# Sample units in another order, value transposes asked for later, and the order of the halves at the start of the output projection

## The chip, the cores and the metric

The kernel runs on one core of one Trainium2 chip. The metric is the device time of one execution in microseconds; of several runs the median is given. The profile is of one more execution, whose own time stands beside its span below.

The core's engines as the profile names them: PE is TensorE (matmuls, PEld its weight loads), DVE VectorE, ACT ScalarE, POOL GpSimd, SP SyncE, which only issues transfers. Each works through its own list of instructions in order and waits at the head of that list.

## The reference, cut to what matters

One decoder layer for two groups of requests that share the weights: a prompt of 1024 tokens and 8 samples of 8 new tokens with a cache of 4096 tokens each. The part around the change is attention and the output projection:

```python
k_cmp = rms_norm(compress(full[:, :, 0], ...), k_gain[0]); v_cmp = compress(full[:, :, 1], ...)
o_cmp, p_cmp = cmp_attention(q, k_cmp, v_cmp, q_pos)
top_i, sel_ok = select_blocks(p_cmp, q_pos, -(-full.shape[1] // SLC_BLOCK))
o_slc = slc_attention(q, top_i, sel_ok, q_pos, full[:, :, 2], full[:, :, 3])
o_win = window_prompt(...)      # or window_sample(...) over the last 512 tokens and the new ones
o_attn = g[..., 0:1] * o_cmp + g[..., 1:2] * o_slc + g[..., 2:3] * o_win
x = x + gate1 * (jnp.concatenate([o_attn, y_conv, y_pool], axis=-1) @ w_out)
h = rms_norm(x, norm2) * (1 + scale2) + shift2
x = x + gate2 * swiglu(h, w_up, w_down)
```

Everything is float32; large products are made of three matmuls on high and low halves.

## The kernel before

The program is written as Python generators, one for each task, and a small planner (`run`, `spawn`, `hold`). The planner keeps an estimated time for each engine (`self.t`, advanced by `use`, `mm` and `tr`). A generator yields the time from which it can go on; of those that can, the planner takes the one with the lowest priority number. This sets the order in which the program is traced. A scheduler with its own model of the engines then sets each engine's list from the traced order and the dependences; `issue_after(x)` adds an edge, so that what is traced inside it comes behind `x` on the engine of `x`.

Three stages follow one another. In the first (to about 370 us) the modulation and the input projection run. In the second, attention, these tasks share TensorE: the last batches of `compress` (the samples' compressed keys and values), the prompt's attention, and the samples' attention. The third (from about 830 us) is the output projection, then the feed-forward part, up and down.

**Prompt attention.** There are 32 units: eight blocks of 128 queries, two halves of the heads, and a branch each (selected with compressed, or window). `scores` (L1078) forms the scores in PSUM, moves them with the mask to `P` on VectorE (L1131), takes the exponential on ScalarE (L1143), and scales by gate and sum on GpSimd (L1153). At its end it spawns `values` (L1161) with the planner's time `ready` at which the last scaling is done. `values` transposes `P` on TensorE in pieces (L144, tile `ident,P`), moves them out as `pt`, and multiplies by the values. The output of a block and half leaves as `mo` (L1223). There are two `P` tiles, and a unit's scores start only when the values of the unit before the last are done (`v_done >= u - 1`).

**Sample attention.** There are 36 units: four pairs of samples, nine units each. Units x = 0 to 7 of a pair are eight parts of the cache, masked by the pair's selected blocks; x = 8 is the sliding window. A unit has a 1 MB tile of keys and values: for x < 8 eight loads of 128 KB each, whose pages come from the page table (L532), for x = 8 one load of 1 MB (L1360). The tiles rotate through two buffers `unit`, and three more, `stream`, from the time when `compress` has given them up; `sample_load` loads the next unit whenever a unit is done. `sample_attention` (L1365) holds a unit until the pair's selection is there (`"at" in st`, set by `sample_select`), then forms scores (`unit,qb` or `stream,qb`), minimum and exponential (`e`); `sample_values` transposes `e` (`ident,e`), moves it to `spt` and multiplies by the values (`unit,spt`, `stream,spt`); the result goes into column `nx` of `part`: 0 to 7 for the selected parts, 9 for the window, 8 and 10 for the new tokens, 11 for the compressed branch. After a pair's ninth unit `sample_combine` (L1427) joins the columns to `co`. For the fourth pair the last step, `sample_store`, happens inside the output projection, at its third weight tile.

**Output projection** (L1540). Eight weight tiles of 512 KB (`w_raw`, three buffers, L1537) are split into high and low halves (`w_hi` on ScalarE, L176; `w_lo` on VectorE or GpSimd, L172). The mixed activations are taken in four quarters of 272 tokens; a quarter is loaded in four pairs of rows (`pair`, L1500 for the first quarter, L1567 for the others) and split into `mh` and `ml` (L176, L172). The groups are quarter 0, quarter 1, then quarters 2 and 3 together; each goes through all eight weight tiles, 24 matmuls a tile and quarter. `mix` splits one pair of rows; the first four belong to the first quarter. `w_raw` lies where `stream` and other tiles of the attention stage lay.

Of the kernel before, what the change touches and what calls it, by code (L numbers as in the profile page):

```python
# [8 lines left out]
F32R = mybir.dt.float32r  # L9
# [8 lines left out]
P = 128  # L18
# [8 lines left out]
HALF = 272  # L27
# [36 lines left out]
class Kernel:  # L64
# [1013 lines left out]
    def scores(self, pool, u, j, half, br):  # L1078
# [10 lines left out]
        if br == "slc":  # L1089
            kj, off = 0, (0 if j < 7 else 64)  # L1090
            seg = [(1, 64 - off, ns)] + ([(0, 0, nc_)] if j < 7 else [])
            lo, hi, mask, m0 = off, 64 + ns, self.m_slc, SEQ - ns - 64
        else:
            kj, off = 1, 64 + w0
            seg = [(2, 0, nw)] + ([(0, nw, nc_)] if j == 7 else [])
            lo, hi = 64 + w0, 64 + ns
# [14 lines left out]
        ready = 0.0  # L1111
        K = self.K[kj]
        for hl in range(2):
# [42 lines left out]
                self.first_evac = self.last_evac  # L1156
                self.scored = True
            yield 0.0
        self.spawn(0, self.values(pool, u, j, half, br, Pt, seg, ready + 0.1))

    def values(self, pool, u, j, half, br, Pt, seg, ready):  # L1161

# [189 lines left out]
            self.unit_next += 1  # L1352

    def sample_fetch(self, u, kv):
        p, x = divmod(u, 9)
        if x < 8:
            for b2 in range(2):
                at = self.gather(kv[:, 4 * b2:4 * b2 + 4], "cacheB", 2 * p + b2, 4 * x, 4)
        else:
            self.nc.sync.dma_start(kv.rearrange("p (b t) f -> p b t f", b=2),  # L1360
                                   self.i["swinKV"][2 * p:2 * p + 2].rearrange("b p t f -> p b t f"))
            at = self.use("dma", 2.9, self.t["pe"]) + 2.5
        return kv.rearrange("p (b t) f -> p b t f", b=2), at

    def sample_attention(self, pool):  # L1365
        nc = self.nc
        self.loads = {}
        self.unit_free = ["unit"] * 2
        self.stream_left = True
        self.unit_next = 0  # L1370
        self.sample_load(pool)
        sts = [{} for _ in range(4)]
        self.spawn(1, self.sample_select(pool, 0, sts[0]))
        for u in range(36):
            p, x = divmod(u, 9)
            st = sts[p]
            if x == 0 and p < 3:
                if p > 0:
                    yield from self.hold(lambda: self.combined >= p)
                self.spawn(1, self.sample_select(pool, p + 1, sts[p + 1]))  # L1380
            yield from self.hold(lambda: "at" in st and u in self.loads and self.u_done >= u - 1)
            kv, at, src = self.loads.pop(u)
            yield max(at, st["at"])
            S = yield from self.bank_of("S")
            for b2 in range(2):
                self.mm(S[self.rows(b2), 0:512], self.qb[:, 2 * p + b2], kv[:, b2, :, 0:P], True, True)
            e = pool.tile([P, 512], F32, name="e", bufs=2)
            nx = x if x < 8 else 9
            v = lambda a: a.rearrange("p (j k) -> p j k", k=64)
            if x < 8:  # L1390
                i1 = st["bias"][:, 8 * x:8 * x + 8][:, :, None].to_broadcast([P, 8, 64])
                nc.vector.tensor_tensor_reduce(out=v(e), in0=v(S[:, 0:512]), in1=i1, scale=-1.0, scalar=3e38,
                                               op0=OP.add, op1=OP.min, accum_out=st["nm"][:, nx:nx + 1])
            else:
                nc.vector.tensor_tensor_reduce(out=e, in0=S[:, 0:512], in1=self.m_win, scale=-1.0, scalar=3e38,
                                               op0=OP.add, op1=OP.min, accum_out=st["nm"][:, nx:nx + 1])
            t = self.use("dve", 0.63, self.t["pe"] + 0.1)
            self.give("S", t)
            nc.scalar.activation(e, e, AF.Exp, scale=-1.0, bias=st["nm"][:, nx:nx + 1],
                                 accum_out=st["den"][:, nx:nx + 1])  # L1400
            t = self.use("act", 0.36, t + 0.1, table="exp")
            self.spawn(2, self.sample_values(pool, u, st, kv, e, nx, t + 0.2, src))
            yield 0.0
# [23 lines left out]
    def sample_combine(self, pool, st, p):  # L1427
        nc = self.nc
        nm, den, part, gr = st["nm"], st["den"], st["part"], st["gr"]

        w = pool.tile([P, 12], F32, name="cw", bufs=2)
        ds_ = pool.tile([P, 4], F32, name="cs", bufs=2)
        dd = pool.tile([P, 12], F32, name="cd", bufs=2)
        br = ((0, 9), (9, 11))
        for x, (a, b) in enumerate(br):
            nc.vector.tensor_reduce(ds_[:, x:x + 1], nm[:, a:b], axis=AX.X, op=OP.min)
        for x, (a, b) in enumerate(br):
            nc.scalar.activation(w[:, a:b], nm[:, a:b], AF.Exp, scale=-1.0, bias=ds_[:, x:x + 1])
        nc.vector.tensor_tensor(dd[:, 0:11], w[:, 0:11], den[:, 0:11], op=OP.mult)
        for x, (a, b) in enumerate(br):  # L1440
            nc.vector.tensor_reduce(ds_[:, 2 + x:3 + x], dd[:, a:b], axis=AX.X, op=OP.add)
        nc.vector.reciprocal(ds_[:, 2:4], ds_[:, 2:4])
        nc.vector.tensor_tensor(ds_[:, 2:4], ds_[:, 2:4], gr[:, 1:3], op=OP.mult)
        for x, (a, b) in enumerate(br):
            nc.vector.tensor_scalar(w[:, a:b], w[:, a:b], ds_[:, 2 + x:3 + x], None, op0=OP.mult)
        o = pool.tile([P, P], F32, name="co", bufs=2) if p < 3 else self.co
        nc.vector.tensor_scalar(o, part[:, 11], gr[:, 0:1], None, op0=OP.mult)
        for c in range(11) if p < 3 else (8, 10, 0, 1, 2, 3, 4, 5, 6, 7, 9):
            nc.vector.scalar_tensor_tensor(o, part[:, c], w[:, c:c + 1], o, op0=OP.mult, op1=OP.add)
        r = self.use("dve", 4.0, self.t["pe"]) + 0.5  # L1450
        if p < 3:
            yield r
            tr = yield from self.bank_of("S")
            self.sample_store(p, tr, o, pool.tile([P, 4, 2, NT], F32, name="smo", bufs=2))
            self.give("S", self.t["dve"])
        self.combined = p + 1
# [83 lines left out]
    def output_projection(self, wp, pool, nt, x1, opened):  # L1540
# [13 lines left out]
        def split():  # L1554
            if raw:
                t, at = raw.pop(0)
                with self.tc.issue_after(self.mix_hi.ins) if self.mix_hi else ExitStack():
                    ws.append([self.piece(wp, self.halves(t[:, x * 512:x * 512 + 512]), at, None) for x in range(2)])
# [11 lines left out]
        def mix(n=1):  # L1570
            for _ in range(n):
                c, k0, t, at = mx.pop(0)
                for k in range(2):
                    hi = pool.tile([P, HALF], F32R, name="mh", bufs=17)
                    lo = pool.tile([P, HALF], F32R, name="ml", bufs=17)
                    r = self.split(hi, lo, t[:, k], HALF, at)
                    parts[c, k0 + k] = (hi, lo, r)

        load()
        load()  # L1580
        split()
        mix(4)
        self.mix_hi = self.last_hi
        load()
# [808 lines left out]
```

## Time and profile before

| | us |
|---|---|
| median of 3 runs (1670.16 to 1675.92) | 1673.87 |
| the profiled execution | 1668.49 |
| its span, first to last instruction | 1666.9 |
| matmuls busy | 1568.7 |
| VectorE busy | 1089.8 |
| ScalarE busy | 779.4 |
| GpSimd busy | 657.6 |

Mean granted TensorE clock over the span: 0.976. The page's slices (40 of 41.7 us each) show TensorE busy at 0.9 or more nearly everywhere but in the first slice; the attention stage is slices 10 to 20:

```profile
PE   6999999998999799988799989999999999899998
PEld 2899997887777466665599979999999999899998
DVE  4713325884645677667489878776777776477767
ACT  3522215335666677656466534443434443344444
POOL 3111011123332233223013366554554555688765
PEclk9999999998999899999899999999999999999999
DMA  9586574425555624233596655446434335977653
```

A row of the view of stretches has the length, then for each engine the busy time with the number of instructions in brackets, the granted clock, the share of the transfer engines that is busy, and GB/s. A row of the order of time has start, duration, engine, line, operation, output and inputs, shape and count, and in brackets the idle time before it and what ended it.

### The profile page before, as it was taken

The numbers are of one execution on the slowest core, as the hardware profiler recorded it, in microseconds if no ns is written. First come the engines' busy times: TensorE is split into PE (matmuls) and PEld (weight loads), VectorE is DVE, ScalarE is ACT, GpSimd is POOL, SyncE is SP. The second block draws the span as 40 slices with busy tenths as digits, with TensorE's granted clock in tenths as the row PEclk, the third lists the DMA queues.
The fourth block names the chain that finished last, engine by engine and source line by source line (L and its number), as shares of the span: only waits on it lengthen the run. The fifth ranks groups of instructions, "written<-read, shape, count | busy, mean of one in ns | idle before, by whom it ended". The sixth has DMA issues, their size and how long they took to land.

```text
span 1666.9 us, 35454 instructions
## 1 busy us (share of the span) xinstructions
PE 1568.7 (94%) x12569; PEld 1390.2 (83%) x12569; DVE 1089.8 (65%) x2641; ACT 779.4 (47%) x1829; POOL 657.6 (39%) x791
## 2 busy tenths in 40 slices
PE   6999999998999799988799989999999999899998
PEld 2899997887777466665599979999999999899998
DVE  4713325884645677667489878776777776477767
ACT  3522215335666677656466534443434443344444
POOL 3111011123332233223013366554554555688765
PEclk9999999998999899999899999999999999999999
DMA  9586574425555624233596655446434335977653
GB/s 342 189 290 173 171 214 150 161 69 163 179 178 169 207 77 131 80 109 106 182 315 215 212 192 181 147 145 208 148 139 142 141 141 196 376 256 249 219 165 125
DMA packets 194658, 302.11 MB, mean 181 GB/s; under 512 B 25841, under 2 KB 131634, under 8 KB 194162
## 3 DMA queue, kind: packets, MB, share of 16 engines
q1 hardware_dynamic: 175346, 272.17, 49.2%
q0 software_dynamic: 6208, 17.38, 3.2%
q10 hardware_dynamic: 12928, 10.29, 2.0%
q8 instruction: 100, 1.64, 0.4%
q14 instruction: 76, 0.62, 0.1%
HBM read 233.43 MB, written 70.53 MB: 182 GB/s over the span
## 4 chain that ended last, share of the span: by engine, by line
PE 41%; DVE 7%; issue 4%; DMA 3%; POOL 2%; ACT 2%; ACTq 0%; DVEq 0%; POOLq 0%; SPq 0%
PE bank L140 40%; PE bank L144 1%; DVE w_lo L172 1%; DVE P L1131 1%; DMA w_raw<-in_wup 1%; DMA w_raw<-in_wout 1%; POOL w_s L172 1%; DMA x<-x_d 1%; ACT w_hi L176 1%; ACT P L1143 1%; POOL b_t L172 0%; DVE b_lo L172 0%; DVE x L1941 0%; POOL f_T L172 0%; DVE f_s L172 0%
## 5 line engine op out<-in xcount | busy, mean ns | idle before, releaser
L140 PE MATMUL bank<-b_hi,w_hi 128*128 128x272 f32 x1232 | 352.2, 291 | 6.8 <-DVE pair L1738 2.9
L140 PE MATMUL bank<-b_lo,w_hi 128*128 128x272 f32 x1232 | 354.4, 289 | 2.5 <-DVE b_lo L172 2.4
L140 PE MATMUL bank<-b_hi,w_lo 128*128 128x272 f32 x1232 | 349.4, 289 | 0.9 <-DVE w_lo L172 0.9
L140 PEld LDWEIGHTS bank<-b_hi,w_hi 128*128 128x128 f32 x1232 | 231.2, 189 | 10.0 <-ACT b_hi L176 4.5
L140 PEld LDWEIGHTS bank<-b_lo,w_hi 128*128 128x128 f32 x1232 | 233.2, 189 | 3.4 <-DVE b_lo L172 3.4
L140 PEld LDWEIGHTS bank<-b_hi,w_lo 128*128 128x128 f32 x1232 | 231.3, 189 | 1.1 <-DVE w_lo L172 1.1
L1153 POOL TENSOR_SCALAR P<-P,st 128x640 f32<-128x640 f32 (+11 forms) x192 | 108.1, 577 | 232.7 <-DVE st L1149 158.3
L172 DVE TENSOR_TENSOR w_lo<-w_raw,w_hi 128x512 fp32r<-128x512 f32 (+2 forms) x120 | 115.8, 972 | 78.6 <-ACT w_hi L176 75.4
L172 POOL TENSOR_TENSOR w_s<-w_raw 128x512 f32<-128x512 f32 (+1 forms) x88 | 126.0, 1432 | 69.3 <-DVE w_lo L172 52.7
L176 ACT ACTIVATE w_hi<-w_raw 128x512 fp32r<-128x512 f32 (+2 forms) x122 | 80.6, 677 | 135.9 <-PE bank L140 82.5
L140 PEld LDWEIGHTS bank<-stream 128*128 128x128 f32 x1056 | 126.6, 198 | 15.3 <-issue 12.8
L140 PE MATMUL bank<-stream 128*128 128x128 f32 x1056 | 133.4, 284 | 2.8 <-DVE pair L589 2.3
L1143 ACT ACTIVATE P<-P,st 128x640 f32<-128x640 f32 (+10 forms) x192 | 112.8, 589 | 47.8 <-DVE st L1131 22.9
L140 PE MATMUL bank<-h_hi,w_hi 128*128 128x384 f32 (+1 forms) x384 | 130.3, 339 | 0.4 <-DVE q L768 0.4
L172 POOL TENSOR_TENSOR x<-x,d_m 128x272 f32<-128x272 f32 x136 | 116.0, 873 | 34.9 <-DVE x L1941 22.4
L140 PE MATMUL bank<-h_hi,w_lo 128*128 128x384 f32 (+1 forms) x384 | 126.3, 329 | 0.0
L140 PE MATMUL bank<-h_lo,w_hi 128*128 128x384 f32 (+1 forms) x384 | 126.3, 329 | 0.0
L140 PE MATMUL bank<-g,w_hi 128*128 128x272 f32 x616 | 120.2, 291 | 5.5 <-DVE x L1941 5.5
L172 DVE TENSOR_TENSOR w_lo<-w_s,w_hi 128x512 fp32r<-128x512 f32 (+1 forms) x124 | 115.5, 934 | 15.1 <-ACT w_hi L176 12.7
L140 PE MATMUL bank<-g,d_hi 128*128 128x272 f32 x616 | 119.2, 290 | 2.2 <-DVE x L1941 0.9
L1941 DVE SCALAR_TENSOR_TENSOR x<-bank,mod,x 128x272 f32<-128x272 f32 (+1 forms) x200 | 90.1, 476 | 40.0 <-PE bank L140 27.5
L1768 POOL TENSOR_TENSOR pair<-pair,f_v 128x272 f32<-128x272 f32 x44 | 44.0, 1000 | 152.0 <-DVE f_v L1738 123.4
(379 smaller groups left out, 3804.4 us busy)
## 6 DMA issues: line engine op xcount, KB each, us to landing
g<-g_d SPq DMA_DIRECT2D x63, 544.0 KB, 6.9
g_d<-f_s SPq DMA_DIRECT2D x57, 544.0 KB, 3.3
wada<-in_wada SPq DMA_DIRECT2D x96, 256.0 KB, 5.4
stream<-in_cacheA SPq DMA_DIRECT2D x192, 128.0 KB, 3.1
w_raw<-in_wup SPq DMA_DIRECT2D x40, 512.0 KB, 4.3
unit<-in_cacheB SPq DMA_DIRECT2D x136, 128.0 KB, 2.4
stream<-in_cacheB SPq DMA_DIRECT2D x120, 128.0 KB, 2.2
w_raw<-in_wout SPq DMA_DIRECT2D x24, 512.0 KB, 5.1
```

Source lines behind the costliest of these rows:

```text
L140: return self.nc.tensor.matmul(out, lhsT, rhs, start=start, stop=stop, skip_group_check=chain)
L144: return self.nc.tensor.transpose(out, in_, self.ident if ident is None else ident)
L172: (self.nc.vector if eng == "dve" else self.nc.gpsimd).tensor_tensor(out, a, b, op=op)
L176: self.last_hi = self.nc.scalar.activation(hi, src, AF.Copy)
L1131: self.last_evac = nc.vector.tensor_tensor_reduce(out=Pt[:, 2 * g + hl, col:col + n], in0=S[g][:, p0:p0 + n], in1=mk, scale=-1.0, scalar=3 ...
L1143: nc.scalar.activation(Ps, Ps, AF.Exp, scale=-1.0, bias=sy[:, g, 0:1], accum_out=sy[:, g, 1:2])
L1153: nc.gpsimd.tensor_scalar(Ps, Ps, sy[:, g, 3:4], 0.0, op0=OP.mult, op1=OP.add)
L1768: nc.gpsimd.tensor_tensor(g[:, 1], s1, v, op=OP.mult)
L1941: self.last_gate = nc.vector.scalar_tensor_tensor(out[:, :n], acc[:, :n], self.mod[:, 5, m, 0:1], out[:, :n], op0=OP.mult, op1=OP.add)
```

## The change

Three edits. In the samples' attention each pair's nine units now run in the order window, then the eight selected parts; the window unit does not wait for the selection, only for the tile that takes its minimum. The combination of the fourth pair adds the window's column before the selected parts' in place of last. In the prompt's attention the planner is told a later time (1.2 in place of 0.1 us after the scaling) for a unit's transposes. In the output projection, the pieces of the second and later quarters are put behind the high half of the first weight tile on ScalarE.

```diff
-        self.spawn(0, self.values(pool, u, j, half, br, Pt, seg, ready + 0.1))
+        self.spawn(0, self.values(pool, u, j, half, br, Pt, seg, ready + 1.2))
...
     def sample_fetch(self, u, kv):
-        p, x = divmod(u, 9)
+        p, x = u // 9, (u + 8) % 9
         if x < 8:
...
         for u in range(36):
-            p, x = divmod(u, 9)
+            p, x = u // 9, (u + 8) % 9
             st = sts[p]
-            if x == 0 and p < 3:
+            if x == 8 and p < 3:
                 if p > 0:
                     yield from self.hold(lambda: self.combined >= p)
                 self.spawn(1, self.sample_select(pool, p + 1, sts[p + 1]))
-            yield from self.hold(lambda: "at" in st and u in self.loads and self.u_done >= u - 1)
+            yield from self.hold(lambda: ("at" if x < 8 else "nm") in st and u in self.loads and self.u_done >= u - 1)
             kv, at, src = self.loads.pop(u)
-            yield max(at, st["at"])
+            yield max(at, st["at"] if x < 8 else 0.0)
...
-        for c in range(11) if p < 3 else (8, 10, 0, 1, 2, 3, 4, 5, 6, 7, 9):
+        for c in range(11) if p < 3 else (8, 10, 9, 0, 1, 2, 3, 4, 5, 6, 7):
...
         def mix(n=1):
             for _ in range(n):
                 c, k0, t, at = mx.pop(0)
-                for k in range(2):
-                    hi = pool.tile([P, HALF], F32R, name="mh", bufs=17)
-                    lo = pool.tile([P, HALF], F32R, name="ml", bufs=17)
-                    r = self.split(hi, lo, t[:, k], HALF, at)
-                    parts[c, k0 + k] = (hi, lo, r)
+                with self.tc.issue_after(self.w_hi.ins) if c else ExitStack():
+                    for k in range(2):
+                        hi = pool.tile([P, HALF], F32R, name="mh", bufs=17)
+                        lo = pool.tile([P, HALF], F32R, name="ml", bufs=17)
+                        r = self.split(hi, lo, t[:, k], HALF, at)
+                        parts[c, k0 + k] = (hi, lo, r)
 
         load()
         load()
         split()
+        self.w_hi = self.last_hi
         mix(4)
```

## The prediction

> **What bounds the kernel now.** I read the page first, then the busy time of each engine by stretch, the waits of TensorE, and the order of time on TensorE, ScalarE, VectorE and SyncE around the places where TensorE stands.
>
> ```profile
> span 1666.9 us, 35454 instructions
> PE 1568.7 (94%) x12569; PEld 1390.2 (83%) x12569; DVE 1089.8 (65%) x2641; ACT 779.4 (47%) x1829; POOL 657.6 (39%) x791
> ```
>
> The reader is to see that the matmul engine is busy for 94% of the span: no edit here takes a matmul away, so a gain can only come out of the 98 us in which it stands, and out of stretches in which it runs at half clock. Two stages are touched. The first is the attention stage, in which the prompt's units and the sample's units share TensorE (busy time by stretch, then TensorE's waits in this stage: total, times, longest):
>
> ```profile
> 373.00:545.00 172.00, 154.44 (x1379) 122.37 (x1379) 91.00 (x429) 105.15 (x312) 54.88 (x120) 0.95 0.58 173
> 545.00:821.00 276.00, 249.72 (x2587) 161.73 (x2587) 180.33 (x744) 168.55 (x438) 75.77 (x114) 0.95 0.41 120
> ```
>
> ```profile
> PE bank L144 <- POOL P L1153: 11.3, 6, 3.6
> PE bank L140 <- DMA unit<-in_swinKV: 6.3, 1, 6.3
> ```
>
> TensorE (first column after the length) is idle for 17.6 us in the first part and 26.3 us in the second. The two waits that the first two edits aim at are 11.3 us on scaled probabilities and 6.3 us on one load of window keys and values. The second stage is the handover from the last sample unit to the output projection, on TensorE and then on ScalarE:
>
> ```profile
> 819.60 1.04 PE L140 MATMUL bank<-stream,spt 128*64 128x128 f32 x16
> 821.53 0.66 PE L144 MATMUL bank<-ident,e 128*128 128x128 f32 x4 [0.89 <-ACT e L1399]
> 824.75 1.98 PE L140 MATMUL bank<-stream,spt 128*64 128x128 f32 x16 [2.56 <-ACT spt L162]
> 830.83 2.18 PE L140 MATMUL bank<-mh,w_hi 128*128 128x272 f32 x8 [4.11 <-ACT w_hi L176]
> ```
>
> ```profile
> 824.12 0.57 ACT L162 ACTIVATE spt<-bank 128x512 f32<-128x512 f32 x1
> 828.06 0.75 ACT L176 ACTIVATE mh<-pair 128x272 fp32r<-128x272 f32 x2 [3.37 <-DMA pair<-mix_d]
> ...
> 830.17 0.61 ACT L176 ACTIVATE w_hi<-w_raw 128x512 fp32r<-128x512 f32 x1
> ...
> 831.21 0.61 ACT L176 ACTIVATE w_hi<-w_raw 128x512 fp32r<-128x512 f32 x1
> ```
>
> TensorE ends the last sample unit at 824.75 + 1.98 = 826.73 and stands 4.11 us until the high half of the first output weight tile exists. ScalarE forms that half at 830.17, but only since its queue has the second quarter's `mh` pieces ahead of it, and those wait until 828.06 for their load. The weights themselves came long before:
>
> ```profile
> L1537 SPq DMA_DIRECT2D w_raw<-in_wout x3: 338/426/432, 820.7 to 821.5; - x3
> ...
> DMA to landing us min/median/max: 4.0/4.8/5.8
> ```
>
> The first tile landed at 820.7 + 4.0 = 824.7, the moment at which ScalarE came free (824.12 + 0.57). The clock follows the stall (columns: length, PE, PEld, DVE, ACT, POOL, granted clock, DMA share, GB/s):
>
> ```profile
> 826.50:829.90 3.40, 0.23 (x4) 0.00 (x0) 1.38 (x5) 1.84 (x7) 0.00 (x0) 0.50 0.77 292
> 829.90:833.30 3.40, 2.40 (x9) 2.08 (x10) 3.37 (x11) 3.40 (x9) 0.00 (x0) 0.50 0.49 134
> 833.30:836.70 3.40, 3.40 (x16) 3.40 (x17) 3.40 (x9) 0.72 (x2) 0.00 (x0) 0.50 0.95 290
> 836.70:840.10 3.40, 3.40 (x29) 3.40 (x29) 1.56 (x4) 1.30 (x3) 1.20 (x1) 0.99 0.88 271
> ```
>
> The first 24 matmuls (tile 0) run from 830.83 to 836.7 at clock 0.50, some 16 in 3.4 us against 29 at full clock; the clock is back after the first stretch in which TensorE is busy throughout.
>
> **The change part by part.** *Second quarter's halves behind the first weight tile's.* It removes and adds no instruction; on ScalarE the two `w_hi` of tile 0 go ahead of the second quarter's `mh`. The pair takes 831.21 - 830.17 = 1.04 us, so it is there at 825.7 and its low halves on VectorE (0.65 us each, idle then) at 827, before TensorE ends the sample at 826.73 plus eight matmuls. So the 4.1 us wait goes. TensorE would be busy from 824.75 on, thus throughout 826.5 to 829.9, and the clock comes back at 829.9: 3.2 us at 16 in 3.4 us make 15 matmuls, the nine left take 9 x 3.4 / 29 = 1.1 us, tile 0 ends at 831.0 in place of 836.7. That is 5.7 us. What is late next is the supply behind it:
>
> ```profile
> 826.70:838.00 11.30, 7.13 (x36) 6.78 (x35) 9.44 (x25) 5.96 (x15) 0.00 (x0) 0.56 0.75 247
> 838.00:865.00 27.00, 27.00 (x217) 26.92 (x216) 19.69 (x39) 15.98 (x33) 3.34 (x3) 1.00 0.96 319
> 865.00:888.00 23.00, 23.00 (x186) 23.00 (x186) 22.27 (x50) 21.05 (x49) 2.82 (x1) 1.00 0.96 311
> ```
>
> From 838 to 888 TensorE is full, so what is gained before is kept if the same bytes and the same vector work fit in less time. The transfer engines have 11.3 x 0.25 + 27 x 0.04 + 23 x 0.04 = 4.8 us free between 826.7 and 888; VectorE has 1.9 + 7.3 + 0.7 = 9.9 us. Transfers are the narrower, so I take **-4.8 us** (bounds -1.4, worked out under the rivals, and -5.7). The `mh` pieces that move back cost nothing: their data comes at 828.06, after the `w_hi` are done. Behind them on ScalarE stands the last sample piece's eviction, which nothing needs before tile 2.
>
> *Sliding unit first.* The same 36 units, matmuls and bytes; the 1 MB window load, one issue, changes places with the eight 128 KB loads of a selected unit, and the window unit of a pair no longer waits for the pair's selection. Two places change. The first is the 6.3 us wait (TensorE; SyncE's issues; landing of the window load in its stretch):
>
> ```profile
> 563.59 1.98 PE L140 MATMUL bank<-unit,qb 128*64 128x512 f32 x4 [6.29 <-DMA unit<-in_swinKV]
> ```
>
> ```profile
> 544.22 10.85 SPq L532 DMA_DIRECT2D stream<-in_cacheB  x18
> 555.17 0.40 SPq L1360 DMA_DIRECT2D unit<-in_swinKV  x1
> ```
>
> ```profile
> DMA to landing us min/median/max: 8.3/8.3/8.3
> ```
>
> The ninth unit's buffer came free at 555.17 and its load took 8.3 us. Now the ninth unit is a selected one. What eight issues cost, with the window load beside them, is in the rows of the end:
>
> ```profile
> 807.87 4.30 SPq L532 DMA_DIRECT2D stream<-in_cacheB  x8
> 812.27 0.84 SPq L1360 DMA_DIRECT2D stream<-in_swinKV  x1
> ```
>
> ```profile
> DMA to landing us min/median/max: 2.1/2.4/6.4
> ```
>
> Eight take 4.30 us to issue and the last lands 2.4 us after its issue: 4.3 - 0.4 + 2.4 = 6.3 us, against 6.4 for the window load there and 8.3 in the stall. So the stall shrinks by 2.0; I take **-1.9 us** (nearest rows), with 0 (another unit meets an 8.3 us load) and -8.0 (all of the 6.3 and, after it, half of 3.4 us at half clock) as ends. The next pair's window load stands in SyncE's queue where eight issues stood, so what is queued behind it goes out some 3.5 us earlier, and I count nothing for it. The second place is the end: the last unit's load is now the eight, as late as the buffer allows; the window load's issue, 0.84 us where 0.40 is usual, shows the buffer free at 812.7, and 812.7 + 6.3 = 819.0 against 812.3 + 6.4 = 818.7: **+0.3 us** (0 to +0.7, if the issue takes 4.3 us in full). The order of additions in the last combination changes nothing in number, and its result is needed only at tile 2.
>
> *Transposes asked for later.* The planner hands out a unit's value part 1.1 us later, so other ready work gets ahead of it in TensorE's order. The longest of the six waits and what stands behind it:
>
> ```profile
> 724.35 1.97 PE L144 MATMUL bank<-ident,P 64*128 64x64 f32 x32 [3.62 <-POOL P L1153]
> 726.26 1.69 PE L144 MATMUL bank<-ident,e 128*128 128x128 f32 x8
> ```
>
> Eight transposes of a sample unit, 0.85 us at full clock, could fill part of it. Of 11.3 us I take **-1.0 us**; the ends are -11.3 and, where the delay lengthens the prompt's own chain, +22 (below). The stretches around that wait say what filling with transposes does for the clock:
>
> ```profile
> 724.10:727.50 3.40, 3.15 (x38) 3.03 (x39) 2.05 (x5) 2.24 (x6) 3.30 (x5) 0.50 0.02 5
> 727.50:730.90 3.40, 3.40 (x40) 2.05 (x40) 1.29 (x2) 1.19 (x2) 0.00 (x0) 1.00 0.00 0
> ```
>
> The first holds transposes alone, and the clock is full right after it: here they count as work. The Trainium skill, TensorE: Matmul & The Clock Gate, section "Part 4: PE-mode transpose", says that transposes do not count as busy time in the same way, so that they would not bring the full clock; by that rule the clock would have stayed low at 727.5, the trace speaks against it, and the term is -1.0 by the rule and up to -2.6 (half of 3.15 us besides) by the rows.
>
> **Sum**: -4.8 - 1.9 + 0.3 - 1.0 = -7.4 us. The profiled execution took 1668.5 us (span 1666.9, 1.6 around it), so 1661.1; the median of the runs is 5.4 us above that execution, so **1666.5 us**.
>
> **The rivals.** Three rows carry them (VectorE; SyncE's waits; outputs of the prompt after 545):
>
> ```profile
> 834.07 1.29 DVE L172 TENSOR_TENSOR w_lo<-w_raw,w_hi 128x512 fp32r<-128x512 f32 x2
> ```
>
> ```profile
> SPq L1537 <- PE bank L140: 5.8, 1, 5.8
> ```
>
> ```profile
> L1223 ACT ACTIVATE mo<-bank x10: 359/383/386, 570.0 to 806.8; 128x256 f32<-128x256 f32 x10
> ```
>
> (A) *A new wait takes the old one's place*: only tile 0 is ordered ahead. If tile 1's `w_hi` stays behind the second quarter's pieces, its low half is there at 834.07 + 1.29 = 835.4 as now, and TensorE, which reached tile 1 at 836.8, gains 1.4 us at most: -1.4 - 1.9 + 0.3 - 1.0 = -4.0, **1669.9**. For it: the edit names one tile. Against: tiles 1 and 2 landed by 821.5 + 5.8 = 827.3, ahead of the quarter's data at 828.06, and their halves come earlier in the program.
>
> (B) *The edit does not do what it says, since the weights come late*: the weight load waited 5.8 us on TensorE, until the next to last sample unit (819.60 + 1.04) had released its buffer. If the turn of the buffers shifts by one, it waits for the last, 826.7; the tile lands at 830.7 and TensorE starts at 831.3, +0.5: +0.5 - 1.9 + 0.3 - 1.0 = -2.1, **1671.8**. For it: the order of units changes; against: five buffers in turn, same number of units.
>
> (C) *Slower: the prompt's chain becomes the bound.* Ten outputs after 545 are 20 units, each of which may start its values 1.1 us later, and the scores two units on wait for them; 20 x 1.1 = 22 us at worst, and 11 if half of them pay, in place of the two gains of this stage: -4.8 + 0.3 + 11 = +6.5, **1680.4**. It decides from some four paying units on (4.5 / 1.1). Against: TensorE is busy 90% of that stretch, so mostly other work is there; and the prompt's last output is at 806.8, 20 us ahead of the stage's end.
>
> **How the numbers follow.** Forecast 0.47, A 0.22, B 0.12, C 0.19. The forecast's own range is -4 to -12 us (1662 to 1670). The range 1659 to 1678 takes in A and B and the nearer part of C. What a measurement of this kernel can tell from no change is about 0.3%, 5 us. Faster by more: 0.42 of the forecast's 0.47 and 0.04 of A and B, 0.46; slower by more: 0.16 of C and 0.02 besides, 0.18; within: 0.36.
>
> **What would show it.** Right: `w_hi` on ScalarE before the `mh` of the second quarter, the wait of TensorE before its first `mh,w_hi` under 1 us, granted clock 1.00 from about 830; the window stall at the ninth unit down to about 4 us; waits on POOL in attention at or under 11 us. Wrong: a wait of TensorE at tile 1 (A), SyncE's first weight load after 826 (B), more than 45 us idle in the attention stage (C), or TensorE no longer full between 831 and 882, which would mean that the supply ate the gain.

## The result and the profile after

The changed kernel takes 1657.0 us (median of 4 runs, 1655.5 to 1658.9) against 1674.9 us of the kernel before (4 runs, 1670.2 to 1679.3): ratio 0.9894, 95% interval 0.9865 to 0.9924, that is 17.9 us less. The forecast was 1666.5, its range 1659 to 1678. The sign was right; the time lies below the range. The profiled execution after took 1656.7 us. From the page after (span, then the busy time of the engines):

```profile
span 1655.1 us, 35447 instructions
...
PE 1570.7 (95%) x12569; PEld 1392.3 (84%) x12569; DVE 1093.6 (66%) x2647; ACT 777.0 (47%) x1824; POOL 657.7 (40%) x791
```

The matmuls are the same 12569. The busy time by stretch, after, for the two stretches shown of before:

```profile
373.00:545.00 172.00, 160.56 (x1475) 128.07 (x1474) 102.35 (x465) 107.00 (x321) 61.53 (x129) 0.96 0.59 177
545.00:821.00 276.00, 248.45 (x2528) 160.07 (x2529) 182.73 (x746) 172.16 (x443) 75.62 (x113) 0.93 0.42 126
```

The number in brackets behind TensorE's busy time is the reading that matters: 1475 matmuls are done by 545 where 1379 were. The second stretch does no better: 2528 against 2587, at clock 0.93 against 0.95. TensorE's waits in attention and at the start of the output projection (370 to 835), after: total, times, longest.

```profile
PE bank L140 <- ACT pt L162: 5.4, 3, 4.0
PE bank L144 <- ACT e L1399: 4.8, 5, 1.6
PE bank L140 <- DMA stream<-in_cacheA: 3.8, 3, 2.7
PE bank L140 <- ACT spt L162: 3.8, 2, 2.7
PE bank L144 <- POOL P L1153: 3.6, 3, 2.0
PE bank L140 <- DVE pt L164: 3.3, 3, 2.9
```

The wait on the window load (6.3 us) and the one on `w_hi` (4.1 us) are no longer in this view, that on scaled probabilities fell from 11.3 to 3.6 us. But waits on `pt` and `spt` have grown: 12.5 us in these three rows, where before ScalarE's two had 4.6 us (2.6 and 2.0) and VectorE's none. The handover to the output projection, order of time on TensorE and on ScalarE, after:

```profile
815.08 0.66 PE L144 MATMUL bank<-ident,e 128*128 128x128 f32 x4 [1.60 <-ACT e L1399]
816.80 1.97 PE L140 MATMUL bank<-unit,spt 128*64 128x128 f32 x16 [1.06 <-ACT spt L162]
818.70 1.88 PE L140 MATMUL bank<-mh,w_hi 128*128 128x272 f32 x8
```

```profile
815.12 1.14 ACT L176 ACTIVATE w_hi<-w_raw 128x512 fp32r<-128x512 f32 x2
...
819.54 0.75 ACT L176 ACTIVATE mh<-pair 128x272 fp32r<-128x272 f32 x2 [1.09 <-DMA pair<-mix_d]
```

The first matmul of the output projection starts at 818.70 in place of 830.83, 12.1 us earlier, without a wait. From there to the end of the span it is 1655.1 - 818.7 = 836.4 us, before 1666.9 - 830.8 = 836.1. So the whole difference between the two executions is made ahead of that matmul. Attention itself began later: the first scores of the prompt (`kh,qh`) start on TensorE at 369.01 before and at 372.19 after. TensorE's list up to there is the same, and the kernel with the edge alone, whose attention is that of before, began it at 372.76; so these 3.2 us are no effect of the change. Attention with the handover went from 461.8 to 446.5 us: 15.3 less, of which 4.1 is the old wait on `w_hi`.

### The profile page after: what moved, and what is told of

Read it like the earlier page. It is cut to its first block, busy times and chain, and to the rows that moved or that the text cites. A ratio compares the mean times of both kernels' runs of the same rounds, so it can differ in the third digit from the quotient of the medians.

```text
span 1655.1 us, 35447 instructions
## 1 busy us (share of the span) xinstructions
PE 1570.7 (95%) x12569; PEld 1392.3 (84%) x12569; DVE 1093.6 (66%) x2647; ACT 777.0 (47%) x1824; POOL 657.7 (40%) x791
## 4 chain that ended last, share of the span: by engine, by line
PE 39%; DVE 4%; DMA 4%; issue 2%; ACT 2%; POOL 2%; ACTq 0%; DVEq 0%; POOLq 0%; SPq 0%
PE bank L140 39%; DVE w_lo L172 1%; DMA w_raw<-in_wup 1%; DMA pair<-mix_d 1%; DMA w_raw<-in_wout 1%; DMA x<-x_d 1%; ACT w_hi L176 1%; ACT P L1143 1%; DVE b_lo L172 0%; POOL w_s L172 0%; DMA x1a<-in_xT 0%; POOL b_t L172 0%; DVE x L1943 0%; POOL f_T L172 0%; DVE f_s L172 0%
## 5 line engine op out<-in xcount | busy, mean ns | idle before, releaser
L1153 POOL TENSOR_SCALAR P<-P,st 128x256 f32<-128x256 f32 (+11 forms) x192 | 108.4, 578 | 237.0 <-DVE st L1149 126.4
L140 PEld LDWEIGHTS bank<-stream 128*128 128x128 f32 x1056 | 129.0, 201 | 16.1 <-issue 11.3
L1143 ACT ACTIVATE P<-P,st 128x128 f32<-128x128 f32 (+11 forms) x192 | 112.8, 588 | 47.1 <-DVE st L1137 24.6
L172 DVE TENSOR_TENSOR w_lo<-w_s,w_hi 128x512 fp32r<-128x512 f32 (+1 forms) x124 | 115.6, 934 | 16.8 <-ACT w_hi L176 11.9
L176 ACT ACTIVATE w_hi<-w_s 128x512 fp32r<-128x512 f32 (+1 forms) x124 | 76.5, 621 | 59.2 <-PE bank L140 34.4
```

The costliest lines, as they stand in the source:

```text
L140: return self.nc.tensor.matmul(out, lhsT, rhs, start=start, stop=stop, skip_group_check=chain)
L172: (self.nc.vector if eng == "dve" else self.nc.gpsimd).tensor_tensor(out, a, b, op=op)
L176: self.last_hi = self.nc.scalar.activation(hi, src, AF.Copy)
L1143: nc.scalar.activation(Ps, Ps, AF.Exp, scale=-1.0, bias=sy[:, g, 0:1], accum_out=sy[:, g, 1:2])
L1153: nc.gpsimd.tensor_scalar(Ps, Ps, sy[:, g, 3:4], 0.0, op0=OP.mult, op1=OP.add)
```

## The experiments

Gain is the median of the kernel before, run on the same chip with the same set, less the kernel's own. Window, later and edge stand for the three edits (sliding unit first; value part asked for later; quarter's pieces behind the first weight tile). "Tail" counts, in TensorE's list, the samples' value matmuls behind the prompt's last product (56 before, 16 after).

| run | what | gain, us | ratio, interval | tail |
|---|---|---|---|---|
| e1 | window alone | 24.0 | 0.9857 (0.983 to 0.9884) | 8 |
| e2 | later alone | 29.6 | 0.9823 (0.9799 to 0.9847) | 8 |
| e3 | edge alone | 6.0 | 0.9966 (0.995 to 0.9982) | 56 |
| e4 | window and later | 19.3 | 0.9892 (0.9871 to 0.9914) | 16 |
| e5 | none; samples' priority 1.9 for 2 | 8.8 | 0.994 (0.992 to 0.9959) | 8 |
| e6 | later, samples' priority falling faster | 20.4 | 0.9879 (0.9857 to 0.9901) | 48 |
| e7 | window, but held for the selection | 2.0 | 0.9988 (0.9974 to 1.0001) | 56 |
| e8 | later and edge | 31.1 | 0.9808 (0.9778 to 0.9837) | 8 |
| e9 | as e8, weights' tiles placed otherwise | 34.0 | 0.9799 (0.9765 to 0.9834) | 8 |
| e10 | later, 0.4 | 15.1 | 0.9904 (0.9876 to 0.9932) | 16 |
| e11 | later, 2.0 | 12.7 | 0.9919 (0.9895 to 0.9944) | 32 |
| e12 | window and edge | 25.1 | 0.9856 (0.9822 to 0.9891) | 8 |
| e13 | later, 0.7 | 17.6 | 0.9874 (0.9843 to 0.9904) | 8 |
| e14 | later, 3.0 | 1.1 | 0.9989 (0.9971 to 1.0007) | prompt last |
| e15 | all three, samples' priority 1.9 | 25.2 | 0.9842 (0.9793 to 0.989) | 8 |
| e16 | the change, one combination moved | 27.9 | 0.9838 (0.9815 to 0.9861) | 16 |
| e17 | the change, beside e16 | 18.0 | 0.9896 (0.9878 to 0.9914) | 16 |

Where an expectation uses a letter, S is an earlier start of the samples that keeps them from being alone at the end, P the waits on scaled probabilities, R chance of the order (each new list lands somewhere), M the balance: samples' work is spent while the prompt has waits to fill.

**Each edit alone, and the two attention edits together.** The edits are those of the diff above, taken singly (e1: the second, e2: the first, e3: the third).

> The sliding unit first, alone. In the changed kernel the samples' first score matmul stands at 397.6 us against 410 (first exponential 404.0 against 434.7), the last prompt output at 814.0 against 806.8 and the samples' last value matmul at about 818 against 826.7. Theory S (the early start keeps the samples from being left alone at the end): first exponential near 404, prompt and samples end within 6 us of each other, and 8 to 13 us faster than before. Theory P (the waits on scaled probabilities were the cost, so the later transposes gained): only the stall on the window load goes, 2 to 4 us faster. Theory R (any new traced order gives another schedule, by chance): anything from 5 us faster to 5 us slower, with no early start needed.

> The later transposes alone. Theory S: within 3 us of before, samples' last value matmul 10 us or more behind the prompt's last output as before. Theory P: waits of TensorE on scaled probabilities fall from 11.3 us to under 4 us, and 7 to 12 us faster. Theory R: anything from 5 us faster to 5 us slower.

> The second quarter's halves behind the first weight tile, alone; attention as before. By the prediction 4.8 us faster (1.4 if tile 1 waits in its place): TensorE's wait of 4.1 us before the first output matmul gone, tile 0 done at about 831 in place of 836.7. In theory R the attention stage comes out the same as before, since nothing traced before the last units changes.

> Window first and later transposes, without the edge on ScalarE. If the three parts add, it lies behind the changed kernel by what the edge alone gains: 4.8 us by the prediction, so about 1662. If the edge's gain depends on how the samples end, it lies elsewhere: with the samples ending beside the prompt, the weights land before ScalarE is free and the edge is worth under 2 us.

Alone they bring 24.0, 29.6 and 6.0 us, the sum of which is three times what the change brings; each attention edit alone is worth more than both together. None of the theories had put the first two above 13 us. The edge adds nothing to the two (1655.8 without it, 1657.0 with it). Order of time on TensorE, then on ScalarE, with window and later but no edge:

```profile
815.88 1.84 PE L140 MATMUL bank<-mh,w_hi 128*128 128x272 f32 x8
```

```profile
812.30 1.14 ACT L176 ACTIVATE w_hi<-w_raw 128x512 fp32r<-128x512 f32 x2
...
816.62 0.75 ACT L176 ACTIVATE mh<-pair 128x272 fp32r<-128x272 f32 x2 [1.11 <-DMA pair<-mix_d]
```

Without the edge there is no wait either. The first half is formed at 812.30, ahead of the second quarter's pieces. Alone, the edge cuts TensorE's wait from 4.11 to 0.95 us (edge alone, TensorE, then ScalarE):

```profile
831.97 2.18 PE L140 MATMUL bank<-mh,w_hi 128*128 128x272 f32 x8 [0.95 <-ACT w_hi L176]
```

```profile
831.07 0.28 ACT L162 ACTIVATE part<-bank 128x128 f32<-128x128 f32 x1 [2.08 <-PE bank L140]
831.29 1.15 ACT L176 ACTIVATE w_hi<-w_raw 128x512 fp32r<-128x512 f32 x2
```

The half now stands behind the eviction of the last sample unit (`part`), which waits for TensorE's last sample product; the forecast had that eviction behind it. The forecast also had the clock come back earlier. It does not: the 24 matmuls of tile 0 take as long as before, from 831.97 to 837.9 against 830.83 to 836.8.

**Is it the tail?** One kernel closes the tail without any of the edits, one opens it again beside the later transposes:

```diff
-        self.spawn(lambda: 2 + 1.1 * self.u_done / 36, self.sample_attention(sp))
+        self.spawn(lambda: 1.9 + 1.1 * self.u_done / 36, self.sample_attention(sp))   # e5
+        self.spawn(lambda: 2 + 1.3 * self.u_done / 36, self.sample_attention(sp))     # e6, with ready + 1.2
```

> The kernel before with one number changed: the samples' attention has priority 1.9 in place of 2 (lower goes first); none of the three edits. In the order of TensorE's list one value product of 8 matmuls of the samples is left after the prompt's last, against 56 before, 16 in the changed kernel and 8 with each of the two attention edits alone. Theory M (what counts is that the samples' work is spent while the prompt still has waits to fill; each attention edit moves the samples forward against the prompt): 15 us or more faster than before, TensorE's waits on scaled probabilities under 4 us. Theory P (it is the later asking for transposes, or the window's load, that takes waits away): within 4 us of before. Theory R (chance of the schedule): anything between.

> The later transposes alone, with the samples' priority rising faster (2 + 1.3 of their progress in place of 2 + 1.1), so that 48 value matmuls of the samples are again left after the prompt's last. Theory M: most of the 29 us is lost, at most 10 us faster than before. Theory P: the later asking keeps its gain, 20 us or more faster than before, and waits on scaled probabilities stay under 4 us.

Closing it brings 8.8 us, opening it (48) takes 29.6 - 20.4 = 9.2 us from the later transposes and leaves 20.4. By these two runs the tail is worth some 9 us and is not the main part. Both also move the rest of the list, so this is no clean price.

**Is it the load or the earlier start?** The window unit again waits for the pair's selection; only the order of the loads stays new:

```diff
-            yield from self.hold(lambda: ("at" if x < 8 else "nm") in st and u in self.loads and self.u_done >= u - 1)
+            yield from self.hold(lambda: "at" in st and u in self.loads and self.u_done >= u - 1)
...
-            yield max(at, st["at"] if x < 8 else 0.0)
+            yield max(at, st["at"])
```

> The sliding unit first, but held for the selection like the others, so that it does not start early: 56 value matmuls of the samples are left after the prompt's last, as before. Theory M: at most 4 us faster than before, with the end of the samples 15 to 20 us behind the prompt's last output. If the order of loads itself were the gain (the 6.3 us wait on the window load): 4 to 9 us faster with the same end.

2.0 us (interval -0.2 to 4.4): the order of loads by itself is worth about what the forecast gave it, and the other 22 us come from not waiting. What that does is in the samples' exponentials on ScalarE, before and then with window alone (count, durations in ns, first and last start):

```profile
L1399 ACT ACTIVATE e<-e,nm x36: 705/721/725, 434.7 to 820.7; 128x512 f32<-128x512 f32 x36
```

```profile
L1399 ACT ACTIVATE e<-e,nm x36: 704/722/727, 403.6 to 807.8; 128x512 f32<-128x512 f32 x36
```

The first sample unit starts 31 us earlier, in a part of the stage in which TensorE otherwise waits for the pieces of `compress`: from 366 to 545 us its waits on `pair` (L624 and L589) come to 10.4 us before and to 1.0 us with window alone.

**The edge without the new order of units, and where the weights lie.**

> Later transposes and the edge on ScalarE, the units in the old order. The later transposes alone came to 1645.6 us with a wait of 6.4 us for the first weight tile's high half. If the edge takes that wait away: 1640 us (1638 to 1643). If the edge is worth little where the samples end beside the prompt (1.2 us the wrong way in the changed kernel): 1644 to 1648.

Later and edge bring 31.1 us, 1.5 more than later alone by the medians, which the two intervals don't tell from nothing. TensorE still waits for `w_hi`, for another reason (TensorE, then SyncE's issues):

```profile
799.09 1.09 PE L140 MATMUL bank<-stream,spt 128*64 128x128 f32 x16
806.49 2.18 PE L140 MATMUL bank<-mh,w_hi 128*128 128x272 f32 x8 [6.31 <-ACT w_hi L176]
```

```profile
800.22 1.34 SPq L1537 DMA_DIRECT2D w_raw<-in_wout  x3
```

The weight load goes out only when the samples' last matmul (799.09 + 1.09) has released the buffer under it. This is rival B of the prediction, and it came with another edit than the one it was tied to: the turn of the buffers shifted. The next kernel lays the slots of the halves over that buffer, and the raw weights elsewhere; an unused slot of each name is asked for first:

```diff
         wp = self.wts = wt_.__enter__()
+        for nm in ("w_hi", "w_lo"):
+            wp.tile([P, 512], F32R, name=nm, bufs=9)
```

> The later transposes and the edge without the new unit order (as in the run before), and the slots of the output weights' halves laid out ahead of those of the raw weights, so that the first weight load no longer lies over the buffer of the samples' last unit. There the load went out at 800.2, 0.02 us after the release by the samples' last matmul, and TensorE stood 6.3 us for the first high half. If that wait is what kept the edge from its gain: the first load goes out before the last matmul, the wait on w_hi falls below 1.5 us, and the time falls by 4 to 8 us below 1643.5 (1636 to 1640). If the output projection is bound by its supply of weights and mixed values anyway: the wait goes, comes back at later tiles, and the time stays within 2 us of 1643.5.

```profile
799.70 1.37 PE L140 MATMUL bank<-mh,w_hi 128*128 128x272 f32 x8 [1.20 <-ACT w_hi L176]
803.06 2.18 PE L140 MATMUL bank<-mh,w_lo 128*128 128x272 f32 x8 [1.99 <-DVE w_lo L172]
```

On TensorE (these rows) the wait falls from 6.31 to 1.20 us, and 1.99 us of a wait on the low half come in its place. The median is 1638.2 us, the lowest of all kernels tried, 34.0 us below before; that it is below e8 the two intervals don't show.

**Window and edge.**

> The sliding unit first and the edge, without the later transposes. Adding: -24 -6 = -30 us, 1645. By the reading that the new unit order has already taken the wait on the first weight tile away (2.3 us of it left with the unit order alone): 1651.2 less at most 2.3, 1649 to 1652, and the wait on w_hi is gone.

The ratio is that of window alone (0.9856 and 0.9857). So with the new order of units the edge is worth nothing that can be measured. (The median, 1647.2 us, lies between the two expectations, on a chip whose kernel before was 2.9 us lower.)

**How much later.** The same line with 0.4, 2.0, 0.7 and 3.0 in place of 1.2.

> The later transposes alone, with a delay of 0.4 in place of 1.2 (before: 0.1). In TensorE's list 16 value matmuls of the samples stand behind the prompt's last product (56 before, 20 or fewer in the change). By the waits (the gain is what TensorE no longer waits for scaled probabilities, and follows the delay): waits on POOL in attention stay above 6 us and the gain is about a third of that of 1.2, -8 to -12 us. By the balance of the samples: -9 for the closed tail, as much as with 1.2 from that part. By chance of the order: the gain lies anywhere between 0 and -30 us, and the waits on POOL don't go with it.

> The later transposes alone, with a delay of 2.0. In TensorE's list 32 value matmuls of the samples stand behind the prompt's last product. By the waits: those on POOL stay at or under 2 us as with 1.2 and the gain stays at -25 to -32 us, less some 3 for the longer tail; by the prompt's chain as bound (rival C of the prediction): the prompt's outputs come later, idle in attention rises above that of 1.2 by 5 us or more, and the gain shrinks to -20 or less. By chance of the order: no relation with 0.4 and 1.2.

> The later transposes alone with a delay of 0.7; 8 value matmuls of the samples stand behind the prompt's last product. By the two counts the gain is 1.83 x (11.3 - W) + 0.147 x 48, with W the waits on scaled probabilities that the trace will show: -24 us if W is 2, -14 if W is 7.5. By chance of the order the gain is not tied to W: off by more than 7 us from that line.

> The later transposes alone with a delay of 3.0. In TensorE's list the samples now end first and 141 transposes and 41 value matmuls of the prompt stand behind their last product. By rival C of the prediction (the prompt's chain becomes the bound): TensorE waits on that chain at the end with nothing beside it, idle in attention is above 45 us, and the gain is under 10 us or gone. If the delay only lets other work pass: W at or under 2 us and a gain of 20 us or more.

From 0.1 on the gain runs 0, 15.1 (0.4), 17.6 (0.7), 29.6 (1.2), 12.7 (2.0), 1.1 (3.0): up to 1.2 and down again (0.4 and 0.7 are not told apart by their intervals). TensorE's waits on scaled probabilities run 11.3, 7.6, 11.7, 1.9, 5.4 and 10.3 us beside it: lowest where the gain is largest, but the gain does not follow them. TensorE's busy time and matmuls in the stretch 373 to 797, which lies within attention in all of these, before, 1.2 and 0.7:

```profile
373.00:797.00 424.00, 382.42 (x3763) 270.95 (x3765) 262.25 (x1148) 263.22 (x723) 130.65 (x233) 0.95 0.47 139
```

```profile
373.00:797.00 424.00, 392.27 (x3927) 274.95 (x3925) 269.43 (x1176) 272.30 (x746) 135.48 (x240) 0.96 0.51 150
```

```profile
373.00:797.00 424.00, 386.94 (x3764) 275.27 (x3765) 264.41 (x1139) 261.26 (x712) 130.17 (x233) 0.94 0.50 150
```

With 1.2 TensorE has done 164 matmuls more by 797 than before. With 0.7 it has done one more, though its attention began 3.9 us later than in the execution of before; more than half of its gain comes after 797, where the tail was. The rule that two counts (waits on scaled probabilities, tail) set the gain falls with e13: its trace shows 11.7 us of waits on scaled probabilities, as many as before, the rule gave 6 us, and 17.6 were measured. With 3.0 the end is rival C (TensorE, a cut of the order of time; the first matmul of the output projection starts only at 836.24):

```profile
812.03 2.93 PE L144 MATMUL bank<-ident,P 64*128 64x64 f32 x49 [2.66 <-DVE st L1131]
817.18 1.08 PE L140 MATMUL bank<-pt,vt__291 128*64 128x256 f32 x8 [2.22 <-ACT pt L162]
```

The samples are through (their last exponential started at 787.5), and the prompt alone goes from wait to wait.

**Why the two don't add.** One place of the change is not in e1, e2, e8 and e12, which have only one of the two attention edits (TensorE, then VectorE, after; then that stretch's busy times and clock):

```profile
640.49 1.98 PE L140 MATMUL bank<-stream,spt 128*64 128x128 f32 x16 [2.73 <-ACT spt L162]
642.39 2.61 PE L144 MATMUL bank<-ident,P 64*128 64x64 f32 x44
647.90 1.97 PE L140 MATMUL bank<-pt,vt__291 128*64 128x256 f32 x8 [2.90 <-DVE pt L164]
```

```profile
641.64 2.36 DVE L1449 SCALAR_TENSOR_TENSOR co<-part,cw,co 128x128 f32<-128x128 f32 x4
...
644.42 2.73 DVE L1449 SCALAR_TENSOR_TENSOR co<-part,cw,co 128x128 f32<-128x128 f32 x5
647.07 1.28 DVE L164 COPY pt<-bank 128x512 f32<-128x512 f32 x2
```

```profile
639.17:656.24 17.07, 12.85 (x98) 8.74 (x98) 9.96 (x32) 6.42 (x15) 5.00 (x6) 0.50 0.21 63
```

The transposes of `P` are through at 645.0 (642.39 + 2.61). Their `pt` stands on VectorE behind a pair's combination, whose result TensorE takes up only at 659.82, and TensorE stands 2.90 us. With the wait for `spt` just before, the clock is at half for 17.07 us, as the last row (a stretch) shows. TensorE is busy for 12.85 of them, so by an estimate from these rows the place costs 2.73 + 2.90 us of standing and up to 12.85 / 2 = 6.4 us of slow work: 12 us at most. Window and later without the edge have it too (2.74 and 2.91 us). First the tail was closed with all three edits in place (priority 1.9, as in e5), which gives another list altogether:

> All three edits, and the priority of the samples' task starting at 1.9 in place of 2: 8 value matmuls of the samples behind the prompt's last product (16 in the change). By the two counts: 1.2 us more than the change from the tail, plus 1.83 per us by which W falls below the change's 3.6: with W at 2, 1653; with W unchanged, 1656. If the two attention edits hurt each other through something else (the earlier start of the samples together with the delay), closing the tail does nothing: 1657, W at or under 3.6.

1649.1 us (four runs, 1641.4 to 1653.9), 7.9 less than the change; the wait of 2.90 us is not in that trace, but much else moved too. Then the place itself was taken away: the second pair's additions come behind the `pt` copies, and in TensorE's list little moves but two transposes.

```diff
+        if p == 1:
+            yield self.t["pe"] + 3.0
+        with self.tc.issue_after(self.last_ev.ins) if p == 1 else ExitStack():   # last_ev: the last vector copy of evac
-        nc.vector.tensor_scalar(o, part[:, 11], gr[:, 0:1], None, op0=OP.mult)
...
+            nc.vector.tensor_scalar(o, part[:, 11], gr[:, 0:1], None, op0=OP.mult)
```

> The change with one thing moved: the second pair's additions (co, VectorE) come behind the three pt copies that stood after them; TensorE's list is the same but for two transposes and one value group, and 16 value matmuls of the samples stay behind the prompt's last product. If that place is what the two attention edits cost each other: the wait of 2.9 us on a pt goes, the 17.07 us at half clock shrink to about 7, and the time falls by 6 to 9 us (2.9 us of idle, and half of the 6.8 to 10 us that TensorE works at half clock no longer). If they fail to add for a reason spread over the stage: the wait goes there and the time stays within 2 us of the change's.

> The changed kernel itself, on the same chip as the run before, as its measure: 1655 to 1659, with the waits of 2.73 us on spt and 2.90 us on pt and the 17.07 us at half clock at the same place, since the lists are fixed.

TensorE and VectorE with the combination moved (its additions now start at 647.10), and the stretch of above:

```profile
641.42 2.51 PE L144 MATMUL bank<-ident,P 64*128 64x64 f32 x42
643.86 1.79 PE L140 MATMUL bank<-pt,vt__291 128*64 128x256 f32 x8
```

```profile
642.57 0.69 DVE L164 COPY pt<-bank 128x512 f32<-128x512 f32 x1 [1.08 <-PE bank L144]
```

```profile
639.17:656.24 17.07, 15.86 (x145) 10.54 (x147) 12.86 (x53) 8.50 (x23) 4.77 (x8) 0.82 0.22 63
```

1647.2 us against 1657.0 for the change on the same chip: 9.8 us for the order of eleven additions, a little above the 6 to 9 expected. In the same 17.07 us TensorE does 145 matmuls where it did 98, and the half clock there lasts 6.83 us. The traces of these two runs put about half of the gain at the place: the same matmul of TensorE's list starts 1.3 us earlier just ahead of it (at 632 us), 6.2 us earlier behind it (at 672). Another 2.8 us come by 770, around two later stretches at half clock that last 3.41 us each in place of 6.83; why they are shorter with the same work is not shown. So a pair's combination in front of the prompt's copies cost the change some 5 us there, and moving it brought 9.8 us in all. Window alone does not have this place, but TensorE waits for two combinations elsewhere (3.87 us at 565.4 and 2.10 us at 671.5). Without the place the change gains 27.9 us, about what either edit gains alone.

Why no more than either? These rows reach from the prompt's first scores to the first matmul of the output projection (before, window alone, later alone, both without the edge); length less TensorE's busy time is its idle time.

```profile
369.00:830.80 461.80, 408.04 (x4000) 287.02 (x3999) 281.40 (x1206) 280.73 (x770) 137.46 (x245) 0.94 0.48 144
371.10:815.80 444.70, 404.19 (x4000) 282.92 (x4000) 284.06 (x1210) 281.51 (x769) 138.61 (x245) 0.95 0.50 146
372.80:810.50 437.70, 399.61 (x4000) 279.50 (x3999) 280.15 (x1212) 281.41 (x773) 138.63 (x245) 0.96 0.51 151
372.60:815.90 443.30, 406.32 (x4001) 285.23 (x4000) 284.08 (x1207) 278.38 (x760) 138.61 (x245) 0.94 0.49 145
```

TensorE is idle for 53.8 us before, 40.5 with window alone, 38.1 with later alone, 37.0 with both. Each edit takes 13 to 16 us of idle time out of the stage, and the other one adds hardly anything: in these traces the two gains are largely the same store of waits, not two. The rest is busy time, which differs for the same 4000 matmuls: 399.6 us with later alone at a clock of 0.96, 406.3 with both at 0.94. These are single executions; that of window alone lies 5 us above its median.

## Why the prediction was wrong

The step that failed is the price of the two attention edits. The sum gave them -2.6 us together (-1.9 + 0.3 - 1.0), each by the wait it aims at; together they bring 19.3 us (e4), and TensorE's idle time in the stage falls by 16.8 us, from waits that the sum doesn't name as well. A second step failed the other way: the terms were added as if each stood on the kernel before. Alone the three edits bring 59.6 us, together 17.9.

- **Second quarter's halves** (forecast -4.8): for the edit alone the size is borne out (6.0 us by the medians; the ratio's interval is 3.0 to 8.4), the mechanism in part: the wait shrinks by 3.2 us, but the clock does not return earlier. In the change it is worth nothing: the new order of units had already brought the first weight load forward, to 804.4, and with it the high half. The signs named for it (`w_hi` ahead of the pieces, no wait at the first `mh,w_hi`) came true, but are also there without the edge, so they could not have shown it.
- **Sliding unit first** (-1.9 and +0.3): right for what was counted, the exchange of the loads (2.0 us measured when the unit is held). Left out was the other half of the edit, no longer waiting for the selection: the samples start 31 us earlier, worth the other 22 us alone. The prediction names it and gives it no term; the sum only asked which stall goes, not what starts sooner. The stall at the ninth unit was to shrink to about 4 us; it is gone. The last combination, counted as nothing, costs 2.02 us: TensorE now comes to it at tile 2 before it is done.
- **Later transposes** (-1.0, ends -11.3 and +22): direction right, size far off, 29.6 us alone. The lower end was wrong too: it took the idle time of the six waits as all there was to win. In that kernel waits on scaled probabilities fell from 11.3 to 1.9 us, but by e6 some 9 us come from the tail; in its trace the stage is 24.1 us shorter, 15.7 of it idle time and 8.4 busy time, of which less is at half clock.
- **Rival C** (slower, prompt's chain the bound): real, but at another dose. At 3.0 it takes the gain away; at 1.2 it does not show.
- **Rival A** named the wrong place. A new wait did take an old one's place, but in the middle of attention, on VectorE's order; moving it away brought 9.8 us.
- **Rival B** came in the two kernels with the later transposes and the old order of units (e2 and e8), not in the change.
- **The step to the median** was sound: 1661.1 + 5.4 is the median of before (1673.9) less the 7.4 us of the sum. By the medians the change brings 16.9 us against that set of runs, 17.9 against the later one, so all of the 9.5 us by which the forecast missed lie in the sum. Between the two profiled executions it is 11.8 us, since that of before was a fast one: its attention began 3.2 us earlier than after.

What stays open: which of the many places where the lists differ make the idle and the slow time, and so why the delay is best near 1.2 and not at 0.7. Over the same stage as in the rows above, TensorE is idle for 38.0, 43.8, 38.1, 52.6 and 54.6 us and busy for 405.6, 408.3, 399.6, 402.2 and 410.3 us with 0.4, 0.7, 1.2, 2.0 and 3.0: 0.7 is behind 1.2 in both.

## What to carry to other kernels

When several edits touch one engine's idle time, ask of each whether its wait is still there after the others, and don't add their gains; run each alone and leave each out. In a list ordered by a planner, an edit is worth what the new list is worth: after every such edit look for the largest new wait, and for work whose result is needed only later (here a combination) standing in front of copies that the matmul engine needs. A time asked for later is a dose with an optimum, to be swept.

## What was not expected of the hardware

Short gaps are enough for half clock. Two stretches at the handover, after:

```profile
813.25:816.66 3.41, 0.89 (x10) 0.42 (x4) 3.31 (x14) 3.41 (x10) 2.82 (x4) 1.00 0.55 150
816.66:820.07 3.41, 3.27 (x22) 2.95 (x23) 3.09 (x9) 1.76 (x5) 0.13 (x1) 0.50 1.03 401
```

In the first of them TensorE is busy 0.89 of 3.41 us, in gaps of which the longest is 1.60 us (the waits of 1.60 and 1.06 us above); the next 3.41 us run at half clock although it is busy for 3.27 of them. The Trainium skill, TensorE: Matmul & The Clock Gate, section "Why this matters for your kernels", asks that no idle gap between bursts of matmuls be longer than about 3 us. The trace does not agree: 1.60 and 1.06 us, with four transposes between them, were enough. Only if the four transposes counted as idle would the gap be 3.32 us, and the prediction's stretch of transposes alone (724.10 to 727.50), with the full clock right after it, speaks against that.

The way back can be longer than one busy stretch. In the 17 us at half clock TensorE works without a gap from 649.41, and the clock is full only at 656.24, two stretches later; before, at the handover, it was full after the first:

```profile
649.41:652.82 3.41, 3.41 (x19) 1.76 (x17) 0.00 (x0) 1.09 (x2) 0.00 (x0) 0.50 0.00 0
652.82:656.23 3.41, 3.41 (x19) 2.12 (x15) 1.16 (x7) 0.96 (x3) 0.00 (x0) 0.50 0.02 5
656.23:659.65 3.42, 3.42 (x41) 2.35 (x40) 2.18 (x14) 2.58 (x8) 0.61 (x2) 1.00 0.01 2
```

By the estimate above, the place with two waits (5.63 us) cost up to twice their length. One list also scatters: with window alone five runs went from 1645.7 to 1656.2 us, with e9's list four from 1637.3 to 1639.6.
